# Remainders of the spilled u blocks moved from GpSimd to VectorE, row gathers pinned in program order

## The chip, the cores and the metric

One core of one Trainium2 chip. The metric is the device time of one launch in microseconds (us). The kernel before takes 2598.91 us (median of three runs, 2596.53 to 2601.98).

## The reference, cut to what matters

Two transformer blocks over 512 tokens of width 1024 in float32. The change lies in the last operation, a product-key memory ("PEER") with 16384 experts. Per token and head (8 heads), the 16 best experts are chosen by two top-16 searches over 128 keys each, and

```python
cand_i = top_i[:, :, 0, :, None] * PEER_N_KEYS + top_i[:, :, 1, None, :]
best_s, best_pos = lax.top_k(cand_s.reshape(t, PEER_HEADS, K * K), K)
idx = jnp.take_along_axis(cand_i.reshape(t, PEER_HEADS, K * K), best_pos, axis=-1)
gate = jax.nn.softmax(best_s, axis=-1).astype(xb.dtype)
h = jax.nn.gelu(jnp.einsum('thkd,td->thk', u_table[idx], xb), approximate=False)
return jnp.einsum('thk,thkd->td', gate * h, v_table[idx])
```

## The kernel before, in words

The function peer (L1747) does this in two ways at once. For the first three tiles of 128 tokens (TD = 384 tokens) it is dense: for each of 128 blocks of 128 experts, TensorE multiplies the block of u with x (function u_block, L1769), ScalarE takes the gelu, VectorE multiplies with a dense matrix of gates G, and TensorE multiplies the result W with the block of v into six PSUM accumulators (py). For the fourth tile it gathers rows: peer_rows (L1712) makes a list of 257 steps, 128 times "gather one row of u for each token (row, L1723) and take its dot product with x (dot)", one step for the weights, and 128 times "gather one row of v and add it, weighted (add)". The gathers are indirect DMAs issued on GpSimd's queue (L1725), 128 rows of 4 KB (512 KB) each, into five rotating buffers.

Float32 products are made of three matmuls (mm3, L47): each operand is split (split, L52) into a high part, copied by ScalarE (L57), and a remainder, raw minus high, by VectorE or, where an engine is handed in, by GpSimd (L58). For a block of u these are u_hi (L57) and u_lo (L58); u_raw, u_hi and u_lo have three buffers each. L49 to L51 are the three matmuls; 24 make one block of u.

Three stages follow one another.
- The **top-k stage**: for each head, TensorE makes the scores and VectorE searches them (top16, L1616 to L1623, and the arithmetic to L1689). After each head 3 to 5 u blocks are computed ahead and stored to DRAM ("spilled", function spill, L1779), 30 in all, with their u_lo on GpSimd.
- The **gate-matrix stage**: for 3 tiles times 16 groups of tokens, peer_scatter (L1692) has VectorE make one-hot matrices in float16 (oh L1699, ohA L1700, two ohB L1704: four instructions of 128x1024 for each group, three buffers of each), TensorE multiplies them (L1710, psx, 16 matmuls for each group) and ScalarE evicts them into Gs (L1712). After every second group one more u block is spilled, 24 in all, in the kernel before with u_lo on GpSimd. Each half tile of Gs goes to DRAM (gd<-Gs, L1825).
- The **v stage**: 6 further u blocks are spilled with u_lo on VectorE (60 in all), the two rows lng and lnb are loaded on GpSimd's queue (L77), and a loop over 128 expert blocks reads G back, loads the spilled block (act<-hd) or makes it (u_block), and multiplies with v. Groups of four spilled blocks alternate with groups of four that are not. The 257 row steps are handed out over this loop, some two to an iteration.

The code is only traced in this order; a scheduler then orders each engine's queue by when it thinks each instruction can start. keep (keep_in_program_order) takes that freedom from one instruction: it stays behind the instruction traced just before it on its engine. In the kernel before the dot and add instructions on VectorE are kept, the gathers are not. So the eight gathers that need no more than head 0's indices, with three dots, stand in the queues of the top-k stage.

Of the kernel before, what the change touches and what calls it, by code (L numbers as in the profile page):

```python
# [27 lines left out]
class Kern:  # L28
# [1685 lines left out]
    def peer_rows(self, sp, x, pk):  # L1714


        nc, I = self.nc, self.I
        t, keep = NT - 1, self.tc.keep_in_program_order
        ix = self.t(sp, [128, 8, 16], U32, "ix")
        g = self.t(sp, [128, 8, 16], F32, "rg")  # L1720
        dots = self.t(sp, [128, 8, 16], F32, "dots")

        def row(name, h, j):  # L1723
            r = self.t(sp, [128, D], F32, "row", 5)
            nc.gpsimd.indirect_dma_start(r, None, I[name], bass.IndirectOffsetOnAxis(ap=ix[:, h, j:j + 1], axis=0))  # L1725
            return r

        def dot(h, j):
            if j == 0:
                nc.vector.scalar_tensor_tensor(ix[:, h], pk[:, t, 0, h], 128.0, pk[:, t, 1, h], OP.mult, OP.add)  # L1730
            r = row("u", h, j)
            keep(nc.vector.tensor_tensor_reduce(r, r, x[:, t, :], 1.0, 0.0, OP.mult, OP.add, dots[:, h, j:j + 1]))  # L1732

        def weights():
            nc.scalar.activation(g, dots, AF.Gelu)
            nc.vector.tensor_tensor(g, g, pk[:, t, 2], OP.mult)
            nc.scalar.activation(x[:, t, :], x[:, t, :], AF.Copy, scale=2.0 ** 0.25)

        def add(h, j):
            r = row("v", h, j)  # L1740
            keep(nc.vector.scalar_tensor_tensor(x[:, t, :], r, g[:, h, j:j + 1], x[:, t, :], OP.mult, OP.add))  # L1741

        picks = [(h, j) for h in range(8) for j in range(16)]
        return [lambda a=a: dot(*a) for a in picks] + [weights] + [lambda a=a: add(*a) for a in picks]


    def peer(self, x):  # L1747

        nc, I, tc = self.nc, self.I, self.tc
        NB, ND = 60, NT - 1  # L1750
        TD = ND * 128
        with ExitStack() as ph:
# [16 lines left out]
            def u_block(b, dst, eng=None):  # L1769

                u = self.load_split(up, I["uT"][b], [128, KC, 128], "u", 3, 3, eng)
                p = self.t(psu, [128, TD], F32, "psu")
                for kc in range(KC):
                    self.mm3(p, [z[:, kc, :] for z in u], [z[:, kc, 0:TD] for z in xT], kc == 0, kc == KC - 1)
                nc.scalar.activation(dst, p, AF.Gelu)  # L1775
# [3 lines left out]
            def spill(n, eng=None):  # L1779
                for b in range(self.ahead, min(self.ahead + n, NB)):  # L1780
                    a = self.t(up, [128, TD], F32, "hs", 2)
                    u_block(b, a, eng)
                    nc.sync.dma_start(hd[b], a)
                self.ahead = min(self.ahead + n, NB)
# [9 lines left out]
            with ExitStack() as sub:  # L1794
                one = sub.enter_context(tc.tile_pool(name="pg1", bufs=1))
                iota2 = self.t(one, [128, 128, 2], F16, "iota2")
                nc.gpsimd.iota(iota2, pattern=[[1, 128], [0, 2]], base=0, channel_multiplier=0, allow_small_or_imprecise_dtypes=True)
                with tc.tile_pool(name="ptk", bufs=2) as wp, tc.tile_pool(name="psk", bufs=1) as kp:
                    sk = self.t(kp, [128, 16, 128], F32, "sk")
                    nc.sync.dma_start(sk, I["sk"])  # L1800
                    iota16 = self.t(kp, [128, 16, NT * 16], BF, "iota16")
                    nc.gpsimd.iota(iota16, pattern=[[1, 16], [0, NT * 16]], base=0, channel_multiplier=0, allow_small_or_imprecise_dtypes=True)
                    for h in range(8):
                        self.peer_topk(wp, h, xT, sk, iota16, pk)
                        spill(5 if h == 7 else 4 - h % 2, nc.gpsimd)
                with tc.tile_pool(name="pgs", bufs=2) as wp:
                    keys = []
                    for t in range(ND):
                        pt = self.psx([128, 3, 128])
                        for i in range(3):  # L1810
                            nc.tensor.transpose(pt[:, i, :], pk[:, t, i].rearrange("p h k -> p (h k)"), self.ident)
                        pkT = self.t(wp, [128, 2, 128], F16, "pkT", ND)
                        nc.vector.tensor_copy(pkT, pt[:, 0:2])
                        gp = self.t(wp, [128, 2, 128], F16, "gp", ND)
                        nc.vector.tensor_scalar(gp[:, 0], pt[:, 2], 2.0 ** 15, None, OP.mult)
                        nc.vector.scalar_tensor_tensor(gp[:, 1], pt[:, 2], 2.0 ** 15, gp[:, 0], OP.mult, OP.subtract)
                        keys.append((pkT, gp))
                    for t in range(ND):
                        for i in range(2):
                            Gs = self.t(wp, [128, 128, 64], F32, "Gs")  # L1820
                            for b in range(8):
                                self.peer_scatter(wp, *keys[t], i * 8 + b, Gs, iota2)
                                if b % 2 == 1:
                                    spill(1, nc.gpsimd)
                            nc.sync.dma_start(gd[2 * t + i], Gs)  # L1825
            spill(NB)
            pss.close()
# [170 lines left out]
```

## Time and profile before

| | |
|---|---|
| median of three runs | 2598.91 us |
| the profiled execution | 2601.8 us |
| its span | 2600.1 us |
| granted TensorE clock, mean | 0.967 |
| PE (TensorE) busy | 2411.4 us (93%) |
| DVE (VectorE) busy | 1997.3 us (77%) |
| ACT (ScalarE) busy | 1129.0 us (43%) |
| POOL (GpSimd) busy | 941.2 us (36%) |
| HBM read, written | 511.99 MB, 51.92 MB |

A row of a group view gives line, engine, operation, tile written and tiles read, shapes and count, then busy time in us and the mean of one in ns, then the idle time just before these instructions and what ended it. A row of a timeline gives start and duration in us, and in brackets the idle time before it.

### The profile page before, as it was taken

How to read it: one execution, taken by the hardware profiler on the slowest of the kernel's cores; microseconds unless marked ns; L12 is line 12 of the kernel's file. 1: busy time of each engine (PE TensorE's matmuls, PEld its weight loads, DVE VectorE, ACT ScalarE, POOL GpSimd, SP SyncE). 2: the span in 40 equal slices, each digit the busy share in tenths (PEclk: the TensorE clock that was granted, in tenths of full speed). 3: DMA queues.
4: the chain of work that ended last, by engine and by line, in shares of the span. 5: the costliest groups of instructions: out<-in, count | busy, mean ns of one | idle time of the engine just before them, and what ended most of it. 6: DMA issues, size and time to landing. Idle time of an engine off the chain costs nothing.

```text
span 2600.1 us, 36041 instructions
## 1 busy us (share of the span) xinstructions
PE 2411.4 (93%) x13302; PEld 1987.8 (76%) x13302; DVE 1997.3 (77%) x3696; ACT 1129.0 (43%) x1660; POOL 941.2 (36%) x674
## 2 busy tenths in 40 slices
PE   6999979999799999899989988899999999999998
PEld 5666666666577787777779878898788879888886
DVE  7698678988866558647699997857788778787886
ACT  3366546777544543224334434443333333332333
POOL 2577422223311103000255456614454434444440
PEclk8999989999899999899999999999999999999999
DMA  7442359999631122115254226689899899999992
GB/s 251 131 153 97 109 198 338 366 358 364 225 110 49 64 70 76 58 58 174 100 165 140 98 78 241 251 325 350 314 352 352 304 335 330 332 324 334 334 321 81
DMA packets 229671, 566.30 MB, mean 218 GB/s; under 512 B 27794, under 2 KB 83138, under 8 KB 228596
## 3 DMA queue, kind: packets, MB, share of 16 engines
q1 hardware_dynamic: 180512, 394.88, 43.4%
q0 software_dynamic: 44176, 159.38, 17.7%
q10 hardware_dynamic: 4804, 9.72, 1.0%
q8 instruction: 105, 1.72, 0.3%
q14 instruction: 74, 0.61, 0.1%
HBM read 511.99 MB, written 51.92 MB: 217 GB/s over the span
## 4 chain that ended last, share of the span: by engine, by line
PE 19%; DVE 12%; issue 12%; POOL 7%; DMA 6%; ACT 1%; SPq 0%; POOLq 0%; DVEq 0%; ACTq 0%
POOL row L1725 5%; PE psu L51 2%; PE psu L49 2%; DMA act<-hd 2%; PE psu L50 2%; DMA row<-in_v,ix 2%; POOL u_lo L58 2%; PE py L50 2%; PE py L51 2%; PE py L49 2%; DVE x L1741 1%; DMA row<-in_u,ix 1%; DVE ohB L1704 1%; PE psb L49 1%; PE psx L1710 1%
## 5 line engine op out<-in xcount | busy, mean ns | idle before, releaser
L51 PE MATMUL psu<-x4T_hi,u_lo 128*128 128x384 f32 x1024 | 347.5, 340 | 18.5 <-POOL u_lo L58 18.5
L49 PE MATMUL psu<-x4T_hi,u_hi 128*128 128x384 f32 x1024 | 350.0, 342 | 0.5 <-ACT act L1775 0.4
L50 PE MATMUL psu<-x4T_lo,u_hi 128*128 128x384 f32 x1024 | 346.5, 338 | 0.0
L50 PE MATMUL py<-v_lo,W_hi 128*128 128x512 f32 x768 | 304.7, 397 | 15.1 <-DVE v_lo L58 15.1
L49 PE MATMUL py<-v_hi,W_hi 128*128 128x512 f32 x768 | 304.1, 396 | 10.9 <-ACT W_hi L57 7.8
L51 PE MATMUL py<-v_hi,W_lo 128*128 128x512 f32 x768 | 304.3, 396 | 1.8 <-DVE W_lo L58 1.8
L1725 POOL DMA_INDIRECT row<-in_v,ix x128 | 185.7, 1450 | 224.4 <-DVE x L1741 192.9
L1725 POOL DMA_INDIRECT row<-in_u,ix x128 | 182.9, 1429 | 228.9 <-DVE dots L1732 203.6
L58 POOL TENSOR_TENSOR u_lo<-u_raw,u_hi 128x1024 fp32r<-128x1024 f32 x54 | 193.7, 3594 | 143.7 <-ACT u_hi L57 143.7
L57 ACT ACTIVATE W_hi<-act 128x384 fp32r<-128x384 f32 x128 | 66.5, 524 | 407.3 <-DVE act L1859 407.3
L58 DVE TENSOR_TENSOR ew_lo<-ew_raw,ew_hi 128x2048 fp32r<-128x2048 f32 x93 | 216.8, 2331 | 34.1 <-ACT ew_hi L57 32.8
L57 ACT ACTIVATE u_hi<-u_raw 128x1024 fp32r<-128x1024 f32 x128 | 134.8, 1055 | 188.3 <-PE psu L50 106.8
L51 PEld LDWEIGHTS psu<-x4T_hi,u_lo 128*128 128x128 f32 x1024 | 195.1, 191 | 19.5 <-POOL u_lo L58 19.4
L49 PEld LDWEIGHTS psu<-x4T_hi,u_hi 128*128 128x128 f32 x1024 | 195.4, 191 | 4.6 <-ACT act L1775 0.8
L50 PEld LDWEIGHTS psu<-x4T_lo,u_hi 128*128 128x128 f32 x1024 | 195.2, 191 | 3.6
L57 ACT ACTIVATE w_hi<-w_raw 128x1024 fp32r<-128x1024 f32 (+1 forms) x103 | 101.8, 992 | 221.0 <-PE psb L50 99.2
L57 ACT ACTIVATE ew_hi<-ew_raw 128x2048 fp32r<-128x2048 f32 x93 | 178.2, 1916 | 42.3 <-PE psa L51 41.3
L50 PEld LDWEIGHTS py<-v_lo,W_hi 128*128 128x128 f32 x768 | 146.7, 191 | 47.9 <-DVE v_lo L58 19.9
L1732 DVE CUSTOM_DVE_ANT_0 row<-row,x 128x1024 f32<-128x1024 f32 x128 | 155.7, 1239 | 34.9 <-DMA row<-in_u,ix 34.8
L1741 DVE SCALAR_TENSOR_TENSOR x<-row,rg,x 128x1024 f32<-128x1024 f32 x128 | 164.0, 1282 | 23.5 <-DMA row<-in_v,ix 21.8
L58 DVE TENSOR_TENSOR v_lo<-v_raw,v_hi 128x1024 fp32r<-128x1024 f32 x128 | 156.3, 1221 | 31.0 <-ACT v_hi L57 30.9
L49 PEld LDWEIGHTS py<-v_hi,W_hi 128*128 128x128 f32 x768 | 146.8, 191 | 41.6 <-ACT W_hi L57 9.8
(667 smaller groups left out, 5862.1 us busy)
## 6 DMA issues: line engine op xcount, KB each, us to landing
u_raw<-in_uT SPq DMA_DIRECT2D x128, 512.0 KB
v_raw<-in_v SPq DMA_DIRECT2D x128, 512.0 KB
ew_raw<-in_wgate SPq DMA_DIRECT2D x32, 1024.0 KB
ew_raw<-in_wup SPq DMA_DIRECT2D x32, 1024.0 KB
ew_raw<-in_wdown SPq DMA_DIRECT2D x32, 1024.0 KB
gd<-Gs SPq DMA_DIRECT2D x6, 4096.0 KB
G<-gd SPq DMA_DIRECT2D x32, 768.0 KB
w_raw<-in_w2b SPq DMA_DIRECT2D x39, 512.0 KB
```

The lines of the kernel that those rows point to most:

```text
L49: mm(out, L[0], R[0], start=start, stop=False)
L50: mm(out, L[0], R[1], start=False, stop=False)
L51: mm(out, L[1], R[0], start=False, stop=stop)
L57: nc.scalar.activation(hl[0], src, AF.Copy)
L58: (eng or nc.vector).tensor_tensor(hl[1], src, hl[0].bitcast(F32), OP.subtract)
L1704: nc.vector.tensor_tensor(B[i], oh, bc(gp[:, i]), OP.mult)
L1710: nc.tensor.matmul(p[:, u, :], A[j], B[i][j], start=i == 0, stop=i == 1)
L1725: nc.gpsimd.indirect_dma_start(r, None, I[name], bass.IndirectOffsetOnAxis(ap=ix[:, h, j:j + 1], axis=0))
L1732: keep(nc.vector.tensor_tensor_reduce(r, r, x[:, t, :], 1.0, 0.0, OP.mult, OP.add, dots[:, h, j:j + 1]))
L1741: keep(nc.vector.scalar_tensor_tensor(x[:, t, :], r, g[:, h, j:j + 1], x[:, t, :], OP.mult, OP.add))
```

## The change

It edits two lines. In the gate-matrix stage, u_lo of the 24 spilled blocks is computed by VectorE and no longer by GpSimd. And every gather is kept in program order on GpSimd's queue.

```diff
         def row(name, h, j):
             r = self.t(sp, [128, D], F32, "row", 5)
-            nc.gpsimd.indirect_dma_start(r, None, I[name], bass.IndirectOffsetOnAxis(ap=ix[:, h, j:j + 1], axis=0))
+            keep(nc.gpsimd.indirect_dma_start(r, None, I[name], bass.IndirectOffsetOnAxis(ap=ix[:, h, j:j + 1], axis=0)))
             return r
```

```diff
                                 self.peer_scatter(wp, *keys[t], i * 8 + b, Gs, iota2)
                                 if b % 2 == 1:
-                                    spill(1, nc.gpsimd)
+                                    spill(1)
                             nc.sync.dma_start(gd[2 * t + i], Gs)
```

## Rows read from the trace of the kernel before

**Rows 1.** Windows by stage: length, each engine's busy us (count), clock, DMA share, GB/s.
```profile
1273.00:1530.00 257.00, 237.95 (x1248) 217.27 (x1247) 238.08 (x1033) 106.69 (x143) 131.29 (x56) 0.96 0.43 140
1530.00:1706.00 176.00, 154.73 (x1330) 146.72 (x1329) 147.08 (x203) 79.97 (x141) 110.01 (x21) 0.93 0.56 210
1706.00:1765.00 59.00, 58.51 (x319) 55.57 (x318) 28.73 (x37) 23.99 (x34) 8.81 (x8) 1.00 0.94 344
1765.00:1780.00 15.00, 12.70 (x53) 9.40 (x52) 11.22 (x19) 4.95 (x7) 3.86 (x4) 1.00 0.87 301
2100.00:2250.00 150.00, 150.00 (x743) 134.30 (x743) 121.74 (x141) 53.72 (x73) 68.33 (x49) 1.00 0.93 333
```

**Rows 2.** Waits of the window 1530 to 1700: total us, times, longest.
```profile
PE psu L51 <- POOL u_lo L58: 18.5, 3, 6.4
```

**Rows 3.** Timeline of GpSimd in the gate-matrix stage.
```profile
1537.90 26.09 POOL L58 TENSOR_TENSOR u_lo<-u_raw,u_hi 128x1024 fp32r<-128x1024 f32 x3 [11.21 <-ACT u_hi L57]
1574.19 2.62 POOL L58 TENSOR_TENSOR u_lo<-u_raw,u_hi 128x1024 fp32r<-128x1024 f32 x1 [3.20 <-ACT u_hi L57]
```

**Rows 4.** Chain of waits, same stage: start, us, engine, tile, line.
```profile
1572.14 0.60 DVE oh L1699
...
1574.55 2.81 DVE oh L1699
...
1599.78 14.31 POOL u_lo L58
...
1691.60 1.86 PE psx L1710 x32
1697.68 1.90 PE psx L1710 x32
1703.80 1.86 PE psx L1710 x32
```

**Rows 5.** Timeline of TensorE: the first psx group, one restart after a wait.
```profile
1536.70 0.30 PE L1710 MATMUL psx<-ohB,ohA 128*128 128x128 f16 x2
...
1614.13 0.69 PE L51 MATMUL psu<-x4T_hi,u_lo 128*128 128x384 f32 x1 [6.06 <-POOL u_lo L58]
```

**Rows 6.** Window around that wait, columns as in rows 1.
```profile
1608.00:1622.00 14.00, 7.94 (x49) 7.71 (x49) 4.29 (x8) 2.53 (x6) 11.02 (x4) 0.76 0.40 124
```

**Rows 7.** Timeline of VectorE: u_lo there, at the end of the gate-matrix stage.
```profile
1700.23 1.21 DVE L58 TENSOR_TENSOR u_lo<-u_raw,u_hi 128x1024 fp32r<-128x1024 f32 x1
...
1704.80 1.23 DVE L58 TENSOR_TENSOR u_lo<-u_raw,u_hi 128x1024 fp32r<-128x1024 f32 x1 [1.55 <-ACT u_hi L57]
```

**Rows 8.** The page's costliest groups: u_lo on VectorE over the whole span.
```profile
L58 DVE TENSOR_TENSOR u_lo<-u_raw,u_hi 128x1024 fp32r<-128x1024 f32 x74 | 90.3, 1221 | 27.3 <-ACT u_hi L57 27.2
```

**Rows 9.** Groups of GpSimd in the top-k stage (1273 to 1530).
```profile
L58 POOL TENSOR_TENSOR u_lo<-u_raw,u_hi 128x1024 fp32r<-128x1024 f32 x33 | 83.7, 2541 | 84.9 <-ACT u_hi L57 84.9
L1725 POOL DMA_INDIRECT row<-in_u,ix x8 | 9.1, 1132 | 5.8 <-DVE pk L1689 3.9 <-issue 1.7 <-DVE tv L1619 0.2
```

**Rows 10.** Chain of waits near the end of the top-k stage.
```profile
1520.08 2.34 DVE ab L1671
```

**Rows 11.** Timeline of GpSimd's queue at the start of the v stage.
```profile
1722.21 0.57 POOL L77 DMA_DIRECT2D lnb<-in_ln_b  x1
1748.34 1.74 POOL L1725 DMA_INDIRECT row<-in_u,ix  x1 [25.57 <-DVE dots L1732]
```

**Rows 12.** Timelines of VectorE, ScalarE, TensorE around the three early dots.
```profile
1327.58 1.23 DVE L1732 CUSTOM_DVE_ANT_0 row<-row,x 128x1024 f32<-128x1024 f32 x1 [0.36 <-DMA row<-in_u,ix]
1329.65 3.50 DVE L1732 CUSTOM_DVE_ANT_0 row<-row,x 128x1024 f32<-128x1024 f32 x1 [0.63 <-DMA row<-in_u,ix]
1333.35 1.20 DVE L1732 CUSTOM_DVE_ANT_0 row<-row,x 128x1024 f32<-128x1024 f32 x1
...
1346.57 0.26 ACT L1685 ACTIVATE pk<-pk 128x64 f32<-128x64 f32 x1 [12.65 <-DVE pk L1684]
...
1351.05 2.07 PE L1639 MATMUL psx<-sk,q 128*128 128x128 f32 x8 [8.56 <-ACT q L1636]
```

## The prediction

> **What bounds the kernel now.** First the windows by stage [rows 1]. In the top-k stage VectorE is busy 238.1 of 257 us and TensorE 238.0: both are nearly full, and the chain of waits runs mostly through VectorE. In the gate-matrix stage TensorE is busy 154.7 of 176 us at a mean granted clock of 0.93, VectorE 147.1, GpSimd 110.0. In the v stage TensorE is full wherever the DMA engines keep up (150.0 of 150 us in 2100 to 2250). So time is won where TensorE stands still.
>
> The waits of the gate-matrix stage name the place: TensorE waits three times for GpSimd's u_lo, 18.5 us in all [rows 2]. The timeline of GpSimd shows why. One u_lo alone takes 2.62 us, but three of them took 26.09 [rows 3], and on the chain a single one stands for 14.31 us [rows 4]: while VectorE issues its float16 instructions one behind another, GpSimd does not get on. The reverse is there too: an oh instruction of 0.60 us takes 2.81 where a u_lo of GpSimd falls on it [rows 4], 2.21 us more. So GpSimd's u_lo is not free for VectorE; it costs VectorE 2.2 us where it gets through, and costs TensorE a wait where it does not.
>
> After each wait TensorE also restarts slowly: in 14 us around the second wait (6.06 us, [rows 5]) the mean granted clock is 0.76 [rows 6], so for 48% of that window it was at 1.2 GHz, the lower of its two levels.
>
> How long would the stage be without these waits? Its last groups of psx start 6.08 and 6.12 us apart [rows 4]; each has 32 matmuls, two of the 48 token groups, with one u block between. 24 such periods of 6.08 are 145.9 us. From the first psx at 1536.70 [rows 5] to the end of the last (1703.80 + 1.86, [rows 4]) it took 169.0. The waits and slow restarts thus cost **23.1 us**, which agrees with 18.5 us of waiting plus 14 x 0.24 = 3.4 us at most of lost clock for each of three.
>
> **The change, part by part.**
>
> *u_lo on VectorE in the gate-matrix stage.* Removed: 24 instructions of GpSimd. Added: 24 on VectorE at 1.22 us, the duration it has there at the stage's end [rows 7] and over the whole span [rows 8]. VectorE's period for one block becomes 8 x 0.60 + 1.22 = 6.02 us, just under TensorE's 6.08. With GpSimd's u_lo getting through it was 8 x 0.60 + 2.21 = 7.01. VectorE's queue is in order, so u_lo can also wait there for ScalarE's u_hi, and the one-hot instructions behind it wait too. Over the span 74 such instructions waited 27.3 us, 0.37 each [rows 8]; one here waited 1.55 [rows 7]. I take 0.37, since it is the mean over 74: 6.39 x 24 = 153.4 us, **15.6 less** than 169.0. The ends: 23.1 less (TensorE's own period), and 24 x (6.02 + 1.55) = 181.7 us, 12.7 more, which is a rival below.
>
> The Trainium skill speaks against this part: "Perfetto Trace Analysis", section "Optimizing Scalar/DVE Operations", says that with a saturated DVE it may make sense to offload work to Scalar or even GPSIMD; it adds that between DVE and GPSIMD, which share a port, this might not help. By the first half the stage would gain nothing (second rival); by the second half it is the sum here. The 2.21 us in the rows side with the second half.
>
> *Three u_lo at the end of the top-k stage.* GpSimd ran 33 of them there [rows 9], the program spills 30, so three belong to the next stage and ran ahead. They held up VectorE on the critical chain (2.34 us for a 128x64 instruction, [rows 10]). Off: 3 x 2.21 = 6.6 us, on: 3 x 1.22 = 3.7 us. I take **-3.0**; the ends are -6.6 (VectorE makes them after this chain) and +3.7 (nothing comes off).
>
> *The kept gathers.* Each names the instruction traced just before it on GpSimd's queue. For the first gather that is the load of lnb, which issues at 1722.21 [rows 11]; later ones follow their predecessor, as the five buffers make them do already. So eight gathers [rows 9] and three dots move from the top-k stage to behind lnb. In the top-k stage the dots and their waits took 0.36 + 1.23 + 0.63 + 3.50 + 1.20 = 6.9 us of VectorE's queue; behind them ScalarE waited 12.65 us for pk, and TensorE 8.56 us for ScalarE [rows 12]. I take **-6.9**, with ends of -3.6 (three bare dots; the 2.2 us in the 3.50 falls on another instruction) and -8.6 (the whole wait of TensorE).
>
> The price lies in the v stage. No SP transfer is behind a gather in its queue, but all share the DMA engines. Eight gathers are 8 x 512 KB = 4.19 MB; at the 344 GB/s of 1706 to 1765 [rows 1] that is 12.2 us of all transfers. What hides it: the next gather of before issued only at 1748.34, 26 us after lnb [rows 11], so five gathers have that time before a dot needs them, and TensorE was busy 58.5 of 59 us there with the DMA share at 0.94. What speaks against hiding: right behind, in 1765 to 1780, TensorE already falls to 12.7 of 15 us [rows 1]. Least: 0, since the stretch 2100 to 2250 shows transfers keeping up with a full TensorE; a gain is excluded, as only work is added. Most: 12.2 plus three dots at 1.22 on VectorE, 15.9. With a row on either side I take half the transfer, **+6.1**; the dots go beside TensorE's work.
>
> **The sum.** The profiled execution took 2601.8 us (span 2600.1). 2601.8 - 15.6 - 3.0 - 6.9 + 6.1 = 2582.4. It lies 2.9 above the median of 2598.91, so on the median's footing **2579.5**.
>
> **The rivals.**
> - *The v stage pays in full.* It runs near the transfer limit, and 15.9 instead of 6.1 gives 2589. For it: 0.94 of the DMA share and the dip behind. Against: the stretches with a full TensorE. On this the skill's page "SBUF — State Buffer" ("A bandwidth-pool intuition that's wrong") calls HBM almost always the end-to-end bottleneck, at some 358 GB/s, by which the gathers would be an estimated 11.7 us; the rows, with TensorE full at 333 GB/s, bear it out in part. Chance 0.15.
> - *VectorE becomes the bound* of the gate-matrix stage: if the 2.2 us do not come off, 147.1 + 24 x 1.22 = 176.4 us fill the 176, and the stage stays as it is. 2579.5 + 15.6 gives 2595, no change to be seen. Against: 2.81 beside 0.60. Chance 0.10.
> - *Slower: u_lo blocks VectorE's queue.* u_hi needs a free buffer, which TensorE frees block by block; if each u_lo stands 1.55 us in VectorE's queue, the stage takes 181.7 us: 2601.8 + 12.7 - 3.0 - 6.9 + 6.1 - 2.9 gives 2608. It decides from a wait of 1.02 us on, where 24 x (6.02 + 1.02) is 169. Against: three buffers let ScalarE run ahead, and VectorE runs up to three token groups ahead of TensorE. Chance 0.07.
> - *The keep moves nothing* (the gathers still stand in the top-k stage). Then -6.9 and +6.1 both fall away: 2580. Chance 0.06; the predecessor named above speaks against it.
>
> **How the numbers follow.** The forecast has 0.62, with 2566 to 2591 as its own range. A measurement of this kernel can tell 0.2%, 5.2 us, from no change, so faster means below 2593.7. The forecast, the first and the last rival are faster (0.83, of which 0.02 lies too high), the second is no change, the third is slower: 0.81, 0.12, 0.07. The range goes from 2564 (the better ends of the two stages before, not all at once) to 2597, above the second rival; the third and the tails are left out.
>
> **What would show it.** Right: no u_lo of GpSimd after 1530 us and no wait of TensorE for one; psx groups about 6.1 to 6.4 us apart throughout; no oh instruction of 2.8 us in the stage; first gathers behind lnb; the wait of TensorE for q in the top-k stage down to some 2 us; more idle TensorE just after the v stage begins. Wrong, if TensorE waits instead for oh, ohA or ohB, if VectorE waits long at u_lo, or if the v stage from lnb to the end is over 10 us longer.

## The result, and the profile after

The changed kernel takes **2566.4 us** (median of 4 runs, 2561.47 to 2569.46) against 2600.44 us (4 runs on the same chip): a ratio of 0.9868, 95% interval 0.9847 to 0.989. It is faster by 34 us; 20 were forecast. The profiled execution took 2568.04 us (span 2566.3), 1.6 above its median.

Where the time went is seen by cutting both spans at the same four events: the start of the top-k stage (the first transposes of x for it, line 1766), the first psx of the gate-matrix stage (line 1710), the end of the last psx, and the first py of the v stage. I call the stretch from the last psx to the first py the hand-over.

| us | start | top-k | gate matrix | hand-over | rest | span |
|---|---|---|---|---|---|---|
| before | 1268.0 | 268.7 | 168.9 | 42.7 | 851.8 | 2600.1 |
| after | 1270.0 | 254.5 | 141.0 | 52.7 | 848.1 | 2566.3 |
| difference | +2.0 | -14.2 | **-27.9** | **+10.0** | -3.7 | -33.8 |

The start is the same code in both, and in the twelve profiles of this document it lies between 1265.9 and 1280.1; the stages behind it repeat better, but a few us in a long stretch of one profile are no evidence.

Windows of after (columns as in [rows 1]): the gate-matrix stage, 100 us in its middle, the hand-over.

```profile
1524.40:1665.60 141.20, 139.52 (x1298) 133.97 (x1297) 140.90 (x214) 79.50 (x140) 0.00 (x0) 1.00 0.70 264
1550.00:1650.00 100.00, 100.00 (x916) 97.48 (x914) 100.00 (x152) 58.16 (x102) 0.00 (x0) 1.00 0.78 295
1666.00:1718.00 52.00, 45.16 (x238) 43.87 (x236) 19.39 (x25) 16.76 (x24) 12.67 (x11) 0.93 0.98 377
```

In the gate-matrix stage TensorE and VectorE are now both busy nearly all the time, GpSimd does nothing, and the granted clock is 1.00, the 2.4 GHz level. The same stage of before, from its first psx to the end of the last:

```profile
1536.70:1705.66 168.96, 147.69 (x1298) 139.83 (x1298) 140.19 (x187) 79.63 (x140) 110.01 (x21) 0.94 0.59 219
```

TensorE idled 21.3 us there (18.5 of them before u_lo [rows 2]) and idles 1.7 now. Its own work took 147.69 us at a clock of 0.94 and takes 139.52 at 1.00. That is 19.6 us of idle time and 8.2 us of slower work, together all of the 27.8 us between the two windows.

The hand-over has the opposite look: TensorE idles 7 of 52 us, the clock falls to 0.93, and the DMA share is at 0.98. The same stretch of before is full:

```profile
1706.00:1748.00 42.00, 41.51 (x238) 40.73 (x237) 14.27 (x17) 16.80 (x24) 1.15 (x2) 1.00 0.93 336
```

The chain of waits of after, at an early, a middle and the last pair of psx starts, in the columns of [rows 4]:

```profile
1542.37 1.86 PE psx L1710 x32
1548.33 1.86 PE psx L1710 x32
...
1560.33 1.86 PE psx L1710 x32
1566.41 1.86 PE psx L1710 x32
...
1657.61 1.86 PE psx L1710 x32
1663.69 1.86 PE psx L1710 x32
```

They stand 5.96 to 6.08 us apart from early to last. In before many stood 6.08 us apart too (psx starts at 1566.90, 1572.98 and 1579.06), but the two around the second wait [rows 5] stood 14.85 us apart (1605.65 and 1620.50).

The tile u_lo of after: instructions, min/median/max in ns, first and last start.

```profile
L58 DVE TENSOR_TENSOR u_lo<-u_raw,u_hi x98: 1205/1218/1226, 1517.9 to 2518.1; 128x1024 fp32r<-128x1024 f32 x98
L58 POOL TENSOR_TENSOR u_lo<-u_raw,u_hi x30: 2396/2410/2841, 1274.9 to 1507.3; 128x1024 fp32r<-128x1024 f32 x30
```

98 on VectorE in place of 74 [rows 8], 30 on GpSimd and none of these after 1507.3. What VectorE waited for at them in the window 1520 to 1666 is one line of the waits (total us, times, longest):

```profile
DVE u_lo L58 <- ACT u_hi L57: 0.3, 1, 0.3
```

GpSimd's queue at the start of the v stage: the first gather now comes right behind the load of lnb, in place of 26 us later [rows 11].

```profile
1682.62 0.55 POOL L77 DMA_DIRECT2D lnb<-in_ln_b  x1
1683.47 1.03 POOL L1725 DMA_INDIRECT row<-in_u,ix  x1 [0.30 <-issue]
```

And TensorE's wait for q in the top-k stage, 8.56 us before [rows 12]:

```profile
1345.79 1.16 PE L1639 MATMUL psx<-sk,q 128*128 128x128 f32 x8 [1.40 <-ACT q L1636]
```

### The profile page after: what moved, and what is told of

Same layout as the page of the kernel before. It is cut to its first block, busy times and chain, and to the rows that moved or that the text cites. A ratio compares the mean times of both kernels' runs of the same rounds, so it can differ in the third digit from the quotient of the medians.

```text
span 2566.3 us, 36046 instructions
## 1 busy us (share of the span) xinstructions
PE 2396.9 (93%) x13302; PEld 1979.6 (77%) x13302; DVE 1988.6 (77%) x3720; ACT 1130.0 (44%) x1660; POOL 823.7 (32%) x650
## 3 DMA queue, kind: packets, MB, share of 16 engines
q1 hardware_dynamic: 180512, 394.88, 43.7%
## 4 chain that ended last, share of the span: by engine, by line
PE 16%; issue 16%; DVE 12%; POOL 8%; DMA 4%; ACT 1%; POOLq 0%; DVEq 0%; SPq 0%; ACTq 0%
POOL row L1725 8%; PE psu L49 2%; PE psu L50 2%; PE psu L51 2%; DMA row<-in_v,ix 2%; PE psx L1710 2%; PE py L50 1%; PE py L51 1%; PE py L49 1%; DMA act<-hd 1%; DVE eq L1676 1%; DVE eq L1680 1%; DVE eq L1678 1%; DVE ti L1623 1%; DVE x L1741 1%
## 5 line engine op out<-in xcount | busy, mean ns | idle before, releaser
L1732 DVE CUSTOM_DVE_ANT_0 row<-row,x 128x1024 f32<-128x1024 f32 x128 | 153.2, 1219 | 46.4 <-DMA row<-in_u,ix 46.4
L51 PEld LDWEIGHTS py<-v_hi,W_lo 128*128 128x128 f32 x768 | 146.1, 190 | 35.5 <-DVE W_lo L58 5.0
```

The lines of the kernel that those rows point to most:

```text
L51: mm(out, L[1], R[0], start=False, stop=stop)
```

## The experiments

Ten kernels. One table holds their stages, cut as above, and their times; "before" ran on the same chip as each.

| | top-k | gate matrix | hand-over | rest | median us (runs) | ratio to before, 95% |
|---|---|---|---|---|---|---|
| before | 268.7 | 168.9 | 42.7 | 851.8 | 2600.44 (4) | 1 |
| after | 254.5 | 141.0 | 52.7 | 848.1 | 2566.40 (4) | 0.9868 (0.9847 to 0.989) |
| e1_keep_only | 261.6 | 169.6 | 50.6 | 846.6 | 2606.76 (10) | 1.0017 (1.0001 to 1.0033) |
| e2_ulo_only | 261.4 | 141.0 | 43.3 | 842.4 | 2561.55 (4) | 0.9854 (0.9827 to 0.9881) |
| e3_late_dots | 255.2 | 141.1 | 47.5 | 829.6 | 2553.12 (6) | 0.9816 (0.9788 to 0.9843) |
| e4_early_rows | 257.3 | 141.0 | 41.9 | 835.5 | 2555.83 (6) | 0.9825 (0.98 to 0.985) |
| e5_two_bufs | 268.4 | 170.8 | 41.6 | 846.6 | 2597.78 (1) | - |
| e6_alternate | 259.3 | 170.6 | 48.0 | 833.1 | 2586.03 (1) | - |
| e7_v_pool | 255.5 | 141.0 | 43.7 | 913.0 | 2632.50 (4) | 1.012 (1.0095 to 1.0145) |
| e8_topk_dve | 252.0 | 141.1 | 47.4 | 840.2 | 2555.92 (4) | 0.982 (0.9786 to 0.9855) |
| e9_index_only | 264.0 | 167.8 | 44.0 | 833.3 | 2586.95 (8) | 0.9944 (0.9919 to 0.997) |
| e10_both | 251.5 | 141.1 | 41.9 | 834.4 | 2545.54 (5) | 0.9796 (0.9772 to 0.9821) |

### Each half of the change alone

e1 keeps the gathers in order and leaves u_lo on GpSimd; e2 is the reverse. Edits against after:

```diff
 # e1_keep_only
-                                    spill(1)
+                                    spill(1, nc.gpsimd)
 # e2_ulo_only
-            keep(nc.gpsimd.indirect_dma_start(...))
+            nc.gpsimd.indirect_dma_start(...)
```

> The gathers are kept, u_lo of the gate-matrix stage stays on GpSimd. If the two halves of the change add up, as the stages of the trace after suggest: the gate-matrix stage (first psx to end of the last) stays at 169 us, the way to the first psx gets some 7 to 10 us shorter (no dots in it), the hand-over from the last psx to the first py gets 10 us longer, and the whole is within 5 us of before, near 2597 us. Rival: the keep brings a large part of the gain, below 2590 us.

> u_lo of the gate-matrix stage on VectorE, gathers free as before. If the halves add up: gate-matrix stage 141 us as after, hand-over 43 us as before, the dots' 7 us still in the top-k stage, near 2568 us in all. Rival: with the dots still in the top-k stage the three u_lo that run ahead make it longer than before, 2575 us or more.

The gate-matrix stage goes with u_lo alone: 169.6 us in e1, 141.0 in e2. The top-k stage splits: -7.1 us with the keep (e1), -7.3 with u_lo (e2), together 14.4, near the 14.2 of after. The longer hand-over goes with the keep: +7.9 in e1, +0.6 in e2. By time the whole gain is u_lo's. The keep alone is no gain (ratio 1.0017, the interval just above 1), and after and e2 can't be told apart (0.9868 and 0.9854).

What the three u_lo did at the end of the top-k stage stands in VectorE's timeline. Before:

```profile
1517.09 2.27 DVE L1669 TENSOR_SCALAR ab<-ab 128x64 bf16<-128x64 bf16 x1
...
1520.00 2.42 DVE L1671 TENSOR_TENSOR ab<-pf,t 128x64 bf16<-128x64 f32 x1
...
1524.42 3.36 DVE L1678 TENSOR_TENSOR eq<-eq,tf 128x1024 bf16<-128x1024 bf16 x1
```

and e2, where they are the only thing changed at this place:

```profile
1517.38 0.18 DVE L1669 TENSOR_SCALAR ab<-ab 128x64 bf16<-128x64 bf16 x1
...
1518.20 0.22 DVE L1671 TENSOR_TENSOR ab<-pf,t 128x64 bf16<-128x64 f32 x1
...
1520.41 1.22 DVE L1678 TENSOR_TENSOR eq<-eq,tf 128x1024 bf16<-128x1024 bf16 x1
```

The same three instructions are 2.09, 2.20 and 2.14 us shorter, 6.4 us in all. VectorE makes the u_lo behind them. One of the three stands on the chain of waits of e2, just ahead of the gate-matrix stage:

```profile
1524.41 1.14 DVE u_lo L58
```

### The hand-over: whose wait is it?

Around the first gathers VectorE's timeline in after reads:

```profile
1684.76 1.23 DVE L58 TENSOR_TENSOR u_lo<-u_raw,u_hi 128x1024 fp32r<-128x1024 f32 x1 [3.24 <-ACT u_hi L57]
...
1692.77 1.23 DVE L1732 CUSTOM_DVE_ANT_0 row<-row,x 128x1024 f32<-128x1024 f32 x1 [6.78 <-DMA row<-in_u,ix]
...
1696.41 1.23 DVE L1732 CUSTOM_DVE_ANT_0 row<-row,x 128x1024 f32<-128x1024 f32 x1 [2.40 <-DMA row<-in_u,ix]
...
1697.56 1.22 DVE L58 TENSOR_TENSOR u_lo<-u_raw,u_hi 128x1024 fp32r<-128x1024 f32 x1
```

The first two dots wait 6.78 and 2.40 us for their rows, and the next u_lo stands behind them in VectorE's in-order queue. TensorE waits for it, and later for ScalarE:

```profile
1698.84 0.44 PE L51 MATMUL psu<-x4T_hi,u_lo 128*128 128x384 f32 x1 [2.52 <-DVE u_lo L58]
...
1712.31 0.44 PE L49 MATMUL psu<-x4T_hi,u_hi 128*128 128x384 f32 x1 [3.64 <-ACT act L1775]
```

ScalarE, which waits for no gather, is late as well, by its own transfer:

```profile
1694.20 1.06 ACT L57 ACTIVATE u_hi<-u_raw 128x1024 fp32r<-128x1024 f32 x1 [3.81 <-DMA u_raw<-in_uT]
```

So there are two prices: the dots in VectorE's queue, and the transfers. e3 lets the dots come later: the row indices of a head, which were made just ahead of its first dot and by a VectorE instruction that is not kept in order, are made in the top-k stage behind the head's pk. e4 does the same and takes the keep off the gathers, so that these may run early while their dots stay in the v stage.

```diff
 # e3_late_dots, against after
         def dot(h, j):
-            if j == 0:
-                nc.vector.scalar_tensor_tensor(ix[:, h], pk[:, t, 0, h], 128.0, pk[:, t, 1, h], OP.mult, OP.add)
...
+        self.row_index = lambda h: nc.vector.scalar_tensor_tensor(ix[:, h], pk[:, t, 0, h], 128.0, pk[:, t, 1, h], OP.mult, OP.add)
...
                         self.peer_topk(wp, h, xT, sk, iota16, pk)
+                        self.row_index(h)
 # e4_early_rows: e3, and
-            keep(nc.gpsimd.indirect_dma_start(...))
+            nc.gpsimd.indirect_dma_start(...)
```

> After, with the indices of all heads computed in the top-k stage, so that the first dots have a predecessor in the loop and stand behind the first v_lo in VectorE's queue; gathers as after. If the 10 us of the hand-over come from VectorE standing at the first two dots (6.8 and 2.4 us) with u_lo behind them, the hand-over falls from 52.7 us by 5 or more, to 2561 us in all. If they come from the 4 MB of rows in front of the u blocks on the DMA engines, it stays within 2 us of 52.7 and the whole at 2566.

> As e3, but the gathers are not kept: five of them stand in the top-k stage again, where the buffers take them, and all dots stay in the v stage. If the transfers are what the hand-over costs: hand-over near 43 us as before, top-k stage as after, 2557 us in all. If the dots are, no different from e3. Rival: five gathers on GpSimd in the top-k stage delay w_lo or u_lo there and the gain is lost, 2566 us.

The hand-over falls from 52.7 us to 47.5 in e3 and to 41.9 in e4. So of the 10.0 us that it had gained, about half (5.2) was the dots in VectorE's queue and the rest the gathers' transfers. e7 below agrees with that: there the first gather issues only 35 us behind the last psx (18 in after), and the hand-over is 43.7 us with the keep in place. The profiles of e3 and e4 differ in span by 12 us (2553.5 and 2541.6), but the medians don't (2553.12 and 2555.83): the profiled execution of e4 is the fastest of its six runs.

There was more in e3 than looked for: **the rest of the v stage** falls from 848.1 to 829.6 us. What VectorE waits for at the dots shows where: the wait groups of the tile row (us, times), in after and in e3. Of the 46.4 us, 9.2 are the two waits in the hand-over that are shown above.

```profile
  DVE row L1732: 46.4, 25
```

```profile
  DVE row L1732: 20.4, 20
```

Is it the indices that were made early, or do they need the other two edits? e9 is before with that edit alone:

```diff
 # e9_index_only: e4, and
-                                    spill(1)
+                                    spill(1, nc.gpsimd)
```

> The kernel before with only the indices of all heads computed in the top-k stage, so that each head's first dot has its predecessor in the loop; u_lo on GpSimd, gathers free. If the shorter v stage of e3 (830 us from the first py to the end instead of 848) comes from dots that no longer run ahead in VectorE's queue, it shows here too: 830 to 836 us there, gate-matrix stage 169 as before, way to the first psx 7 us shorter, 2577 us in all. If it needs u_lo on VectorE, or was chance, the v stage stays at 845 to 852 us and the whole at 2590 or more.

The rest falls to 833.3 us in e9 too, with u_lo on GpSimd and no keep, and the median by 13 us (2586.95 against 2599.79, ratio 0.9944), less than expected but outside the error. In the profiles 4.7 us of the gain lie in the top-k stage, which has lost the early dots here as well. The waits of the v stage (from 1748 us in before, 1710 in e9), total, times and longest, in before:

```profile
DVE row L1732 <- DMA row<-in_u,ix: 33.8, 23, 4.5
```

and in e9:

```profile
DVE row L1732 <- DMA row<-in_u,ix: 19.5, 19, 2.7
```

So it is a separate improvement. What the code suggests, and no run tried by itself: a kept instruction follows the one traced just before it; a head's first dot was traced behind its index instruction, which itself was free to move, and the dots came with it, ahead of their rows.

### What the loss in the gate-matrix stage was

The prediction had two accounts of it: 2.2 us on VectorE for each u_lo of GpSimd that gets through, and a long wait of TensorE where it does not. If GpSimd gets on only when VectorE stands still, then VectorE's lead over TensorE (three buffers each of oh, ohA and ohB) sets how long a u_lo is held. e5 is before with two buffers each. e6 is e3 with every second u_lo of the stage back on GpSimd:

```diff
 # e5_two_bufs, against before
-        oh, A = (self.t(wp, n, F16, x, 3) for x in ("oh", "ohA"))
+        oh, A = (self.t(wp, n, F16, x, 2) for x in ("oh", "ohA"))
...
-            B.append(self.t(wp, n, F16, "ohB%d" % i, 3))
+            B.append(self.t(wp, n, F16, "ohB%d" % i, 2))
 # e6_alternate, against e3
-                                    spill(1)
+                                    spill(1, nc.gpsimd if b % 4 == 1 else None)
```

> The kernel before (u_lo on GpSimd, gathers free) with two instead of three buffers of oh, ohA and ohB. Theory: GpSimd gets on only when VectorE stands still with full buffers, so with fewer buffers VectorE stops sooner, the longest u_lo falls clearly below 21 us and TensorE's wait for u_lo below 18.5 us, while VectorE pays its 2.2 us for more of the 24 (24 x 7.01 = 168), so that the stage stays near 169 us: the loss only changes its place. Rival: the wait of TensorE is the whole loss, and the stage gets shorter with it, 155 us or less; or the long u_lo have nothing to do with VectorE's run and stay at 14 to 21 us.

> e3 with every second u_lo of the gate-matrix stage on GpSimd again (12 of 24). If VectorE pays 2.2 us for each that gets through, two blocks cost it 8 x 0.60 x 2 + 1.22 + 2.21 = 13.0 us against TensorE's 12.2, and the stage takes 12 x 13.0 = 156 us, half way between 141 and 169. Rival: with VectorE's run broken by its own u_lo, GpSimd is not held up at all and the stage stays at 141 to 146 us.

**e5.** With less lead, TensorE's long waits for u_lo fall to one of 6.9 us (18.5 at three places before [rows 2]), but TensorE now waits for ohB as well. Waits of e5, window 1530 to 1710:

```profile
PE psx L1710 <- DVE ohB L1704: 11.0, 16, 2.3
...
PE psu L51 <- POOL u_lo L58: 6.9, 1, 6.9
```

The stage stays at 170.8 us, as the theory had it. That the loss has only changed its place isn't shown by this: fewer buffers may make TensorE wait for ohB by themselves, and no run has two buffers with u_lo on VectorE. The timeline of GpSimd in e5 has, once, three u_lo that last as long together as those of before did [rows 3], and the first of them takes 21.77 us: the longest u_lo did not get shorter, although the theory had said that it would.

```profile
1545.88 26.42 POOL L58 TENSOR_TENSOR u_lo<-u_raw,u_hi 128x1024 fp32r<-128x1024 f32 x3 [5.05 <-ACT u_hi L57]
```

Later in the stage the theory does better: the longest u_lo of e5 there take 6.3 to 9.0 us, where before has two more of 20.9 and 20.3.

**e6.** Half of the instructions on GpSimd cost the whole gain: the gate-matrix stage takes 170.6 us, as if all 24 were there. No theory had that. It is one run, but the stage repeats well: 141.0 to 141.1 us in the seven kernels that have these u_lo on VectorE, 167.8 to 170.8 in the four that have all of them on GpSimd. GpSimd's timeline shows one u_lo held and one not:

```profile
1541.20 18.57 POOL L58 TENSOR_TENSOR u_lo<-u_raw,u_hi 128x1024 fp32r<-128x1024 f32 x1 [16.00 <-PE psx L1710]
...
1566.97 2.92 POOL L58 TENSOR_TENSOR u_lo<-u_raw,u_hi 128x1024 fp32r<-128x1024 f32 x1 [7.20 <-PE psx L1710]
```

VectorE's timeline of e6 shows what it did in the first:

```profile
1548.51 1.24 DVE L58 TENSOR_TENSOR u_lo<-u_raw,u_hi 128x1024 fp32r<-128x1024 f32 x1
...
1556.87 0.71 DVE L1699 TENSOR_TENSOR oh<-iota,pkT 128x1024 f16<-128x1024 f16 x1
...
1566.95 0.69 DVE L1700 TENSOR_TENSOR ohA<-iota,pkT 128x1024 f16<-128x1024 f16 x1 [9.38 <-PE psx L1710]
```

It ran without a gap until 1557.6 us, then stood still 9.38 us. GpSimd's u_lo ended at 1559.77, 2.2 us after VectorE fell silent, about the length of one undisturbed u_lo (2.41 us). A float32 u_lo of VectorE at 1548.51 in the midst of the stretch did not let it in. TensorE stood before that u_lo for 9.30 us, and for 24.1 in the whole stage, which is nearly all of its idle time there (it is busy 146.45 of 170.61 us, at a clock of 0.91). Timeline of TensorE in e6, then its waits (1530 to 1700):

```profile
1559.82 0.69 PE L51 MATMUL psu<-x4T_hi,u_lo 128*128 128x384 f32 x1 [9.30 <-POOL u_lo L58]
```

```profile
PE psu L51 <- POOL u_lo L58: 24.1, 3, 9.3
```

The held u_lo of before end as the one of e6 does. Timelines of GpSimd and VectorE in before, around the second of the three:

```profile
1593.14 20.94 POOL L58 TENSOR_TENSOR u_lo<-u_raw,u_hi 128x1024 fp32r<-128x1024 f32 x1 [4.09 <-ACT u_hi L57]
...
1621.59 0.69 DVE L1704 TENSOR_TENSOR ohB<-oh,gp 128x1024 f16<-128x1024 f16 x1 [9.71 <-PE psx L1710]
```

VectorE fell silent at 1611.88 us, and the u_lo ended at 1614.08, again 2.2 us later. The other two, of 21.46 and 20.34 us, ended 2.2 us behind VectorE's stop as well.

So the loss doesn't go by the number of u_lo on GpSimd: three waits of TensorE for held ones cost as much in e6 as the three of before [rows 2]. That speaks for the second account (a u_lo of GpSimd that is held stops TensorE) and against a sum of 2.2 us each. VectorE did pay: in before twelve one-hot instructions took 2.9 us in place of 0.7, some 26 us in all. But TensorE waited only 2.8 us for one-hot matrices in the whole stage. Why one u_lo is held for 18.57 us and another gets in at once was not settled; [rows 3] have both kinds as well.

### Other places for the same exchange

Does any stream of VectorE hold GpSimd back? e7 puts the u_lo of the v stage, where VectorE's work is float32, on GpSimd. And is GpSimd worth keeping for the 30 u_lo of the top-k stage? e8 gives these to VectorE, which is nearly full there.

```diff
 # e7_v_pool, against e3
-                        u_block(b, a)
+                        u_block(b, a, nc.gpsimd)
 # e8_topk_dve, against e3
-                        spill(5 if h == 7 else 4 - h % 2, nc.gpsimd)
+                        spill(5 if h == 7 else 4 - h % 2)
```

> e3 with u_lo of the 68 blocks made in the v stage on GpSimd. If VectorE's float32 instructions with two operands hold GpSimd up and are held up as its float16 ones are, VectorE gives 68 x 1.22 = 83 us away and takes up to 68 x 2.2 = 150 us on, TensorE waits more for u_lo or v_lo, and it is slower than e3 by 10 us or more, 2563 us or above. Rival: only the float16 forms are concerned; VectorE (80% busy there) is relieved, TensorE's 10 us of waiting for v_lo go, 2545 us.

> e3 with the 30 u_lo of the top-k stage on VectorE too. VectorE bounds that stage: 30 x 1.22 = 36.6 us more, less the 2.2 us that come off where a GpSimd u_lo fell on eq, cand or ab. If most of them fall on searches that they don't hold up, it is slower by 15 to 37 us, 2568 to 2590 us. Rival: all locks come off, three or so a head, 8 x 3 x 2.2 = 53 us, and it is faster than e3, 2537 us.

**e7** is slower than before (ratio 1.012), and in the opposite way to the gate-matrix stage. GpSimd is hardly held. The tile u_lo in e7:

```profile
L58 POOL TENSOR_TENSOR u_lo<-u_raw,u_hi x98: 2339/2407/3490, 1277.5 to 2578.9; 128x1024 fp32r<-128x1024 f32 x98
```

but VectorE is. Groups of VectorE in the window 1725 to 2540 (columns as in [rows 8]), e7 and then e3:

```profile
L58 DVE TENSOR_TENSOR v_lo<-v_raw,v_hi 128x1024 fp32r<-128x1024 f32 x115 | 200.7, 1746 | 20.5 <-ACT v_hi L57 19.7 <-DMA act<-hd 0.8
```

```profile
L58 DVE TENSOR_TENSOR v_lo<-v_raw,v_hi 128x1024 fp32r<-128x1024 f32 x126 | 154.0, 1222 | 24.5 <-ACT v_hi L57 24.5
```

The same v_lo takes 1746 ns on the mean in place of 1222, and the rest of the span 913.0 us in place of 829.6. Part of that is seen in the same window: TensorE's waits for v_lo go from 10.3 us to 35.3, while VectorE's waits for rows of u hardly move (18.9 to 23.1). Whether GpSimd gets in because the work is float32, or because VectorE leaves gaps (it is busy 668.6 of 815 us), these runs do not separate.

**e8** costs VectorE almost nothing. Groups of VectorE by form in the window 1285 to 1525, e3:

```profile
L1676 DVE TENSOR_TENSOR eq<-iota,ab 128x1024 bf16<-128x1024 bf16 x15 | 25.6, 1708 | 0.0
```

and e8:

```profile
L58 DVE TENSOR_TENSOR u_lo<-u_raw,u_hi 128x1024 fp32r<-128x1024 f32 x31 | 38.7, 1248 | 4.2 <-ACT u_hi L57 4.2
...
L1676 DVE TENSOR_TENSOR eq<-iota,ab 128x1024 bf16<-128x1024 bf16 x16 | 13.2, 825 | 0.0
```

The window as a whole (columns as in [rows 1]), e3 and then e8:

```profile
1285.00:1525.00 240.00, 231.89 (x1223) 211.97 (x1222) 223.71 (x1013) 104.01 (x140) 114.83 (x45) 0.98 0.37 124
```

```profile
1285.00:1525.00 240.00, 235.20 (x1254) 215.23 (x1253) 227.13 (x1061) 101.81 (x134) 38.41 (x15) 0.99 0.38 123
```

31 u_lo add 38.7 us to VectorE, and yet its busy time in that window goes only from 223.7 to 227.1: its own instructions get shorter, this eq from 1708 to 825 ns. The top-k stage is 3 us shorter (255.2 to 252.0). The medians of e8 and e3 (2555.92 and 2553.12) can't be told apart, so for the whole kernel this edit is no loss, and no gain is shown.

### What adds up

e10 joins them: u_lo on VectorE in both stages, the early indices, no keep on the gathers.

```diff
 # e10_both: e4, and
-                        spill(5 if h == 7 else 4 - h % 2, nc.gpsimd)
+                        spill(5 if h == 7 else 4 - h % 2)
```

> e4 (u_lo of the gate-matrix stage on VectorE, five gathers in the top-k stage, all dots in the v stage) with the 30 u_lo of the top-k stage on VectorE as in e8. If the stages add up: way to the first psx 252 to 254 us, gate-matrix stage 141, hand-over 42, v stage 833, 2545 us in all, some 2% below before. If the gains of e4 and e8 are the same time counted twice, no better than e3 at 2553.

Its stages are those of its parts: top-k 251.5 (e8: 252.0), hand-over 41.9 (e4: 41.9), rest 834.4 (e4: 835.5). The median of 2545.54 us, ratio 0.9796, is the lowest of all, clear of before and after; its interval still overlaps those of e3, e4 and e8.

## Why the prediction was right, and where its sizes were off

The direction, the place and the main mechanism (TensorE's waits for GpSimd's u_lo, and the slow clock behind them) were right, and 2566.4 lies in the range of 2564 to 2597, near its lower end. The terms:

- **u_lo in the gate-matrix stage: -15.6 forecast, -27.9 measured.** Two steps were mis-sized. First, "24 such periods of 6.08 are 145.9" counts a whole u block in each period. The stage holds fewer. The matmuls of psu with u_lo in it, in after:

```profile
L51 PE MATMUL psu<-x4T_hi,u_lo 128*128 128x384 f32 x177 | 59.6, 337 | 0.2 <-DVE u_lo L58 0.2
```

  A block has 8 of these, so 177 are 22.1 blocks, and before has as many. TensorE's first six token groups run 2.4 us apart with no whole block between:

```profile
1524.48 0.28 PE L1710 MATMUL psx<-ohB,ohA 128*128 128x128 f16 x2
...
1526.89 0.28 PE L1710 MATMUL psx<-ohB,ohA 128*128 128x128 f16 x2
```

  At the 6.08 - 1.86 = 4.2 us that a block takes in a period, the missing 1.9 are 8 us: the floor was some 138, an estimate from these rows, not 145.9; the stage took 141. Second, "I take 0.37" for VectorE's wait for u_hi: it was 0.3 us in the whole stage, not in each block. Of the 12.3 us between 153.4 and 141.1, 7.4 come from this second step (24 x 0.31, VectorE's 6.39 in place of TensorE's 6.08) and the rest from the first. With the floor too high the loss came out as 23.1 where 28 were there. The prediction's own check would have warned of it: 18.5 us of waits and three times up to 3.4 us of lost clock are 28.7, and it passed as agreement with 23.1. TensorE's slower work was 8.2 us, 2.7 for each of the three.
- **Three u_lo at the end of the top-k stage: -3.0 forecast, -7.3 measured** (e2). It goes past the lower end of -6.6. Three instructions lost 6.4 us together, near the 6.6 of the prediction. Of the 3.7 us that had been set against them for the u_lo on VectorE, one u_lo of 1.14 us stands on this chain. That makes 5.3; the other 2 us are not accounted for.
- **The dots out of the top-k stage: -6.9 forecast, -7.1 measured** (e1), by the wait that was named: TensorE's 8.56 us for q is 1.40.
- **The v stage: +6.1 forecast, +6.3 measured** (hand-over +10.0, rest -3.7). The sum agrees; the way there was half right. The transfers share the path, as said. But "the dots go beside TensorE's work" failed: VectorE's queue is in order, a dot that waits for its row holds the u_lo behind it, and e3 got 5.2 us of the 10.0 back. And the -3.7 is no part of the mechanism: the rest of e1 and e2 differs from before by -5.2 and -9.4, so in the five kernels without the early indices it scatters from 842.4 to 851.8 us. So the agreement of the sum is partly luck.

Sum of the four: -19.4 forecast. The stages of after give -27.9 - 14.2 + 6.3 = -35.8, and with the +2.0 of the start -33.8.

**The rivals.** That VectorE would become the bound fell in its price: VectorE is full in the stage (140.90 of 141.20 us), but so is TensorE, and the 2.2 us did come off. That u_lo would block VectorE's queue fell with the 0.3 us. That the keep moves nothing fell with the first gather behind lnb. That the v stage pays in full was the nearest: the hand-over alone paid 10.0 of 15.9.

The prediction weighed the Trainium skill, "Perfetto Trace Analysis", section "Optimizing Scalar/DVE Operations": offloading from a full VectorE, with the reserve that between these two engines it might not help. The runs decide for the reserve. Here the offloading did harm: -27.9 us when it was undone, and all of it back when half was restored (e6, one run).

## What to carry to other kernels

An instruction given to GpSimd is not free because GpSimd idles: look at its duration beside VectorE's stream, and if one instruction takes 18 us (e6) where alone it takes 2.4, give it back to VectorE, even a VectorE that seems full, and measure the stage. When a floor is built as so many periods of a repeating pattern, count the instructions in the stage first, since work before and after it may carry part of the pattern. An instruction that waits for a transfer in an in-order queue is charged with all that stands behind it: keep it late, and look what instruction a kept order is tied to.

## What the runs showed of the hardware

- **GpSimd beside float16 on VectorE.** A 128x1024 u_lo that alone takes 2.41 us took 18.57 us (e6), and three of before took 20.3 to 21.5, behind VectorE's back-to-back instructions of 0.60 us; each ended 2.2 us after VectorE stopped. Twelve others of before got in at once, and each made one VectorE instruction 2.2 us longer; what decides between the two was not found. The Trainium skill, "SBUF — State Buffer", section "SBUF: two separate sides", says that of a GpSimd instruction that reads SBUF and a VectorE instruction with two SBUF inputs, whichever starts first has their shared pair of ports for the whole instruction and the other is fully blocked. The 2.81 us of an oh [rows 4] agrees with that for VectorE; for GpSimd the runs differ: it was held for a long row of VectorE's instructions, not for one.
- **GpSimd beside float32 on VectorE** (e7): there GpSimd gets through (longest u_lo 3.49 us, median 2.41), and VectorE pays, v_lo 1222 to 1746 ns on the mean. VectorE's stream has gaps there, so the runs do not show that the type decides.
- **A nearly full VectorE took on more work at almost no cost** (e8): 38.7 us of u_lo added, 3.4 us of busy time more, since its other instructions were shorter without GpSimd beside them (eq 1708 to 825 ns).
- **Half of an offload can cost as much as all of it** (e6, one run: 170.6 us with 12 on GpSimd, 168.9 with 24).
